# Softmax results and retention outputs transposed in 32x32 blocks by VectorE and moved over DRAM, in place of TensorE transposes

## The chip, the cores and the metric

The kernel runs on one core of one Trainium2 chip. The metric is device time in microseconds (us) for one execution of the whole program; lower is better. PE is TensorE, DVE is VectorE, ACT is ScalarE, POOL is GpSimd, and SP is the engine that only issues transfers (its queue is SPq in the trace).

## The reference, cut to what matters

Two layers of a block with neighbourhood attention and retention side by side, then a third block of another kind. Sequence 512, width 1024, all fp32. In each of the two layers the parts that the change touches are these:

```python
# neighbourhood attention: 8 heads of 64
s = einsum('bhcd,bhrckd->bhcrk', q_row, k_win) * scale + bias
pr = softmax(s)                                # one row per query
out = einsum('bhcrk,bhrckd->bhcd', pr, v_win)  # sums over keys
# bidirectional retention: 4 heads, values of 256
o = (o - mu) * rsqrt(var + GN_EPS)
yb = silu(g) * o
merged = sigmoid(gate_a) * (ya @ w_branch_a) + sigmoid(gate_b) * (yb @ w_branch_b)
```

The softmax is computed with queries on the 128 partitions, but the product with the values sums over keys, so keys must lie on the partitions there. The retention output is computed with tokens on the partitions, but `yb @ w_branch_b` sums over features. Both results have to be transposed in between.

## The kernel before, in words

Every product is made of three fp32r matmuls on a high and a low part of each operand (`mm3`). `split` (line 667) makes the two parts of a tile: ACT casts the high part, DVE subtracts it from the source for the low part. Weights come in as `raw` tiles of 512 KB and are split by the same two engines into `whi` and `wlo`; four `raw` buffers are shared by the weights and by `pth`/`ptl`.

In each layer the main line of PE's work is, in this order: `vg` of head 0, `q`, `k`, `v` of the attention, then for each of four retention heads `qr` and `vg`, then `ba`, `ga`, and pairs of `gb` and `bb`. Beside it run generators of side work: `attention()` (line 1167) and one `retention(h, qk)` (line 1255) per head. `attention()` must be finished before `ba`, which reads its result; the retention outputs are read only by `bb`.

For each of eight attention heads there are two halves (`gp`). A half is: four matmuls into a PSUM bank `s`; DVE adds the bias and takes the row maximum (`nmx`); ACT makes the exponential with its row sums; DVE takes the reciprocal and scales the tile `s_` (128x512, queries by keys). Then, at lines 1225 to 1230, PE transposes the four 128x128 blocks of `s_` into a PSUM bank `pt`, and `split` reads `pt` into `pth` and `ptl`. After both halves, eight matmuls `o` multiply `pth` and `ptl` with the values. In `retention`, the two tiles `yt` of a head (each 128x512, tokens by features) are transposed by PE at lines 1300 to 1306 into two banks `ybt` and split into `ybh` and `ybl`.

No engine's order is written by hand. All instructions are recorded by a `Planner`, which gives each a cost (`record`, line 309) and a due time, plays all engines through, and issues them in the order that it found. Each engine then runs its own list strictly in that order. The costs that matter here:

```python
if op.dma:
    op.cost = 1.0 if eng == "gpsimd" else 0.06
    op.set = n * o.ap[0][1] * 4 / 3.6e5
elif meth == "transpose":
    op.cost = 0.11
```

A transfer is taken to land 2.0 us after its bytes have passed, an instruction may follow one of another engine after `SYNC = 0.5`, and one of PE after `PE_SYNC = 1.5`.

Of the kernel before, what the change touches and what calls it, by code (L numbers as in the profile page):

```python
# [12 lines left out]
F32 = mybir.dt.float32  # L13
# [5 lines left out]
P = 128  # L19
# [487 lines left out]
def block_kernel(ctx: ExitStack, tc: tile.TileContext, keys, w, x, xt, pt, bias, decay, tabs, vecs,  # L507
# [16 lines left out]
    def nm(s):  # L524
        uid[0] += 1
        return f"{s}{uid[0]}"
# [4 lines left out]
    def tmp(s="tmp", dt=F32):  # L531
        return tp.tile([P, 512], dt, tag="tmp", name=nm(s))
# [7 lines left out]
    def psb(s="ps"):  # L540
        return pp.tile([P, 512], F32, tag="bg", name=nm(s), bufs=4)
# [4 lines left out]
    ident = cst.tile([P, P], F32, name="ident")  # L546
# [120 lines left out]
    def split(src, hi, lo):  # L667
        S.copy(out=hi, in_=src)
        V.tensor_tensor(out=lo, in0=src, in1=hi.bitcast(F32), op=ALU.subtract)
# [31 lines left out]
    def to_feature_half(src, xt_, t, hf):  # L701
# [6 lines left out]
        S.copy(out=h, in_=v)  # L708
        V.tensor_tensor(out=l, in0=v, in1=h.bitcast(F32), op=ALU.subtract)

    def bcast(r):
        b = [act(s="bc") for _ in range(2)]
        for hf in range(2):
            G.dma_start(out=b[hf], in_=rows[r:r + 1, hf * HALF:(hf + 1) * HALF].to_broadcast([P, HALF]))
        return b
# [30 lines left out]
    ps = psb("warm")  # L746
# [337 lines left out]
    for i in range(DEPTH):  # L1084
# [82 lines left out]
        def attention():  # L1167
# [14 lines left out]
            for f in range(4):  # L1182
# [5 lines left out]
                for h in (2 * f, 2 * f + 1):  # L1188
# [8 lines left out]
                    for gp in range(2):  # L1197
# [24 lines left out]
                        for u in range(2):  # L1222
                            V.tensor_scalar(out=s_[:, u * 256:u * 256 + 256], in0=s_[:, u * 256:u * 256 + 256],
                                            scalar1=sm[:, u:u + 1], scalar2=None, op0=ALU.mult)
                        pst = psb("pt")
                        for c in range(4):
                            src = c ^ 1 if gp == 1 and c > 1 else c
                            TE.transpose(out=pst[:, c * P:(c + 1) * P], in_=s_[:, src * P:(src + 1) * P], identity=ident)
                        ps2 = slice(512 * gp, 512 * gp + 512)
                        split(pst, pth[:, ps2], ptl[:, ps2])  # L1230
                        yield 2.2
                    po = psb("o")
                    for n in (1, 2, 3, 0):
# [21 lines left out]
        def retention(h, qk):  # L1255
# [41 lines left out]
            yield 1.0  # L1297
            while not att_done:
                yield 0.1
            for c in range(2):  # L1300
                ps = psb("ybt")
                for n in range(4):
                    TE.transpose(out=ps[:, n * P:(n + 1) * P],
                                 in_=yb[n // 2][:, 256 * (n % 2) + P * c:256 * (n % 2) + P * c + P], identity=ident)
                hi, lo = act(F32R, "ybh"), act(F32R, "ybl")
                split(ps, hi, lo)
                ybT[2 * h + c] = (hi, lo)
                yield 0.5

        att_done = []  # L1310
        att_gen = attention()
# [418 lines left out]
```

## Time and profile before

| | |
|---|---|
| Median of 3 runs | 2258.62 us (2257.99 to 2259.11) |
| The profiled execution, its own time | 2257.85 us |
| Its span | 2256.1 us |
| PE busy | 2228.9 us (99% of the span) |
| DVE busy | 1467.0 us (65%) |
| ACT busy | 1038.2 us (46%) |
| POOL busy | 635.1 us (28%) |

Times of instructions come from the one profiled execution; its own time is 1.75 us longer than its span, and 0.77 us shorter than the median. In the trace all instructions have line 503, where the planner issues them, so groups are told apart by the names of their tiles: `pt` are the softmax transposes, `ybt` those of the retention, `qks` the attention's operands moved by SP.

### The profile page before, as it was taken

To read this page: it belongs to the slowest core of one execution; us is meant where nothing else is said; L and a number is where in the kernel's file an instruction comes from. 1 tells how busy PE (TensorE), PEld (TensorE's weight loads), DVE (VectorE), ACT (ScalarE), POOL (GpSimd) and SP (SyncE) were. 2 spreads that over 40 slices of the span, in tenths; PEclk is the share of its full clock that TensorE was granted. 3 is DMA by queue.
4 is the path that set the end of the run, shared out by engine and by line. 5 is a ranking of instruction groups with operands and counts; after the bars stand their busy time and mean duration, and the time that the engine had idled before them with its cause. 6 is when DMAs were issued, how large, how long until landed. Compare 5 with 4: busy or idle time off the path is not lost.

```text
span 2256.1 us, 28362 instructions
## 1 busy us (share of the span) xinstructions
PE 2228.9 (99%) x10572; PEld 1863.2 (83%) x10572; DVE 1467.0 (65%) x2139; ACT 1038.2 (46%) x1680; POOL 635.1 (28%) x752
## 2 busy tenths in 40 slices
PE   9999999999999999999999999999999979999998
PEld 8888888888888888888888888888888868888887
DVE  4488734576887867277853474787887874566663
ACT  5378632244444444267752333544443674333332
POOL 0011011147437830011001136636761230221220
PEclk9999999999999999999999999999999999999999
DMA  7344333433333444444333433333343432333331
GB/s 242 88 125 144 121 94 94 141 100 122 121 101 102 124 138 135 121 127 134 115 94 100 159 101 104 98 116 101 121 143 119 145 120 77 103 103 103 103 99 51
DMA packets 85017, 262.14 MB, mean 116 GB/s; under 512 B 10880, under 2 KB 11024, under 8 KB 84880
## 3 DMA queue, kind: packets, MB, share of 16 engines
q1 hardware_dynamic: 79680, 242.16, 34.8%
q0 software_dynamic: 5200, 18.18, 2.7%
q8 instruction: 83, 1.36, 0.2%
q14 instruction: 54, 0.44, 0.1%
HBM read 235.13 MB, written 12.58 MB: 110 GB/s over the span
## 4 chain that ended last, share of the span: by engine, by line
PE 86%; DVE 6%; POOL 4%; ACT 2%; issue 1%; DMA 1%; DVEq 0%; SPq 0%; ACTq 0%; POOLq 0%
PE up L503 15%; PE tm L503 14%; PE vg L503 8%; PE fd L503 7%; PE u L503 6%; PE g L503 5%; PE ga L503 4%; PE bb L503 4%; PE gb L503 4%; PE qr L503 4%; PE ro L503 2%; PE ba L503 2%; PE k L503 2%; PE q L503 2%; PE v L503 2%; DVE wlo L503 2%
## 5 line engine op out<-in xcount | busy, mean ns | idle before, releaser
L503 DVE TENSOR_TENSOR wlo<-raw,whi 128x1024 fp32r<-128x1024 f32 (+1 forms) x372 | 497.7, 1345 | 337.2 <-ACT whi L503 334.9
L503 ACT CAST whi<-raw 128x1024 fp32r<-128x1024 f32 (+1 forms) x372 | 385.6, 1041 | 349.5 <-PE fd L503 74.8
L503 PE MATMUL up<-xtl,whi 128*128 128x512 f32 x704 | 271.2, 390 | 0.0
L503 PE MATMUL up<-xth,wlo 128*128 128x512 f32 x704 | 271.2, 390 | 0.0
L503 PE MATMUL up<-xth,whi 128*128 128x512 f32 x704 | 270.8, 389 | 0.0
L503 DVE SCALAR_TENSOR_TENSOR h<-up,vec,h 128x511 f32<-128x511 f32 x176 | 130.8, 745 | 88.0 <-ACT h L503 86.3
L503 PEld LDWEIGHTS up<-xth,whi 128*128 128x128 f32 x704 | 132.2, 188 | 27.3
L503 PEld LDWEIGHTS up<-xth,wlo 128*128 128x128 f32 x704 | 132.1, 188 | 27.4
L503 PEld LDWEIGHTS up<-xtl,whi 128*128 128x128 f32 x704 | 132.1, 188 | 27.2
L503 PE MATMUL fd<-whi,gh 128*128 128x512 f32 x336 | 132.3, 394 | 0.5 <-DVE mid L503 0.3
L503 PE MATMUL fd<-wlo,gh 128*128 128x512 f32 x336 | 132.2, 394 | 0.0
L503 PE MATMUL fd<-whi,gl 128*128 128x512 f32 x336 | 131.8, 392 | 0.0
L503 POOL TENSOR_TENSOR ws<-raw,raw 128x512 f32<-128x512 f32 x48 | 76.2, 1606 | 197.2 <-DMA raw<-in_w 197.2
L503 POOL TENSOR_TENSOR h<-h,h 128x512 f32<-128x512 f32 x44 | 78.2, 1777 | 160.3 <-DVE h L503 114.5
L503 ACT ACTIVATE h<-up,vec 128x512 f32<-128x512 f32 x88 | 68.0, 776 | 111.9 <-PE up L503 111.9
L503 POOL DMA_DIRECT2D bias<-in_bias x30 | 16.5, 549 | 321.9 <-DVE s L503 321.9
L503 PE MATMUL u<-xtl,whi 128*128 128x512 f32 (+1 forms) x288 | 101.4, 356 | 1.7 <-DVE xtl L503 1.7
L503 PE MATMUL u<-xth,wlo 128*128 128x512 f32 (+1 forms) x288 | 101.6, 356 | 0.0
L503 DVE TENSOR_TENSOR x<-x,fd 128x512 f32<-128x512 f32 x144 | 96.0, 680 | 8.4 <-PE fd L503 8.2
L503 PE MATMUL u<-xth,whi 128*128 128x512 f32 (+1 forms) x288 | 100.7, 356 | 0.0
L503 PE MATMUL vg<-whi,xtl 128*128 128x512 f32 x256 | 100.5, 395 | 0.0
L503 POOL TENSOR_TENSOR ws<-raw,ws 128x512 f32<-128x512 f32 x48 | 74.3, 1568 | 92.3 <-DMA raw<-in_w 92.2
(347 smaller groups left out, 5636.3 us busy)
## 6 DMA issues: line engine op xcount, KB each, us to landing
raw<-in_w SPq DMA_DIRECT2D x376, 512.0 KB, 3.9
bias<-in_bias POOLq DMA_DIRECT2D x30, 256.0 KB, 3.9
bc<-in_rows POOLq DMA_DIRECT2D x22, 256.0 KB, 6.4
qks<-kh SPq DMA_DIRECT2D x32, 128.0 KB, 2.4
qks<-kl SPq DMA_DIRECT2D x32, 128.0 KB, 2.4
dec<-in_tabs POOLq DMA_DIRECT2D x7, 448.0 KB, 3.6
raw<-in_w SPq DMA_DIRECT2D x8, 256.0 KB, 5.5
xr<-in_xt SPq DMA_DIRECT2D x8, 256.0 KB, 5.6
```

The source lines that it names most:

```text
L503: getattr(getattr(self.nc, op.eng), op.meth)(*op.args, **op.kw)
```

## The change

A new function `turn(src_, parts)` (line 711 of the changed file) takes the place of the transposes. DVE transposes the tile in blocks of 32x32 into a buffer `tb`: one instruction where the order of the key blocks is kept, three where the second half swaps two of them. SP writes `tb` to a DRAM tile `turn` (256 KB), then reads it back in four transfers of 64 KB, each to 32 partitions in runs of 512 bytes, into the tile that was the source. `split` then reads this tile in SBUF in place of a PSUM bank. In the retention the splits are made in halves of 256 columns. The PSUM banks `pt` and `ybt` are gone.

```diff
+    def turn(src_, parts):
+
+        b = tmp("tb")
+        for lo_, order in parts:
+            n = len(order)
+            v = src_.rearrange("p (c b j) -> p b c j", c=4, b=4)
+            V.transpose(out=b.rearrange("p (b c i) -> p b c i", b=4, c=4)[:, :, lo_:lo_ + n],
+                        in_=v[:, :, order[0]:order[0] + n])
+        d = dp.tile([P, 512], F32, name=nm("turn"))
+        Q.dma_start(out=d, in_=b)
+        for k in range(4):
+            Q.dma_start(out=src_[32 * k:32 * k + 32].rearrange("p (a n) -> p a n", a=4),
+                        in_=d.rearrange("(a j) (b n) -> b j a n", a=4, b=4)[k])
+        return src_.rearrange("p (a c i) -> p c a i", a=4, c=4)
...
-                        pst = psb("pt")
-                        for c in range(4):
-                            src = c ^ 1 if gp == 1 and c > 1 else c
-                            TE.transpose(out=pst[:, c * P:(c + 1) * P], in_=s_[:, src * P:(src + 1) * P], identity=ident)
+                        got = turn(s_, ((0, (0, 1, 2, 3)),) if gp == 0 else ((0, (0, 1)), (2, (3,)), (3, (2,))))
                         ps2 = slice(512 * gp, 512 * gp + 512)
-                        split(pst, pth[:, ps2], ptl[:, ps2])
+                        split(got, *(v[:, ps2].rearrange("p (c a i) -> p c a i", c=4, a=4) for v in (pth, ptl)))
...
+            got = [turn(yb[n2], ((0, (0, 1, 2, 3)),)) for n2 in range(2)]
+            yield 0.2
             for c in range(2):
-                ps = psb("ybt")
-                for n in range(4):
-                    TE.transpose(out=ps[:, n * P:(n + 1) * P],
-                                 in_=yb[n // 2][:, 256 * (n % 2) + P * c:256 * (n % 2) + P * c + P], identity=ident)
                 hi, lo = act(F32R, "ybh"), act(F32R, "ybl")
-                split(ps, hi, lo)
+                for n2 in range(2):
+
+                    split(got[n2][:, c:4:2], *(v[:, 256 * n2:256 * n2 + 256].rearrange("p (u a i) -> p u a i", u=2, a=4)
+                                              for v in (hi, lo)))
                 ybT[2 * h + c] = (hi, lo)
-                yield 0.5
+                yield 0.2
```

`V` is VectorE, `Q` is SP's queue. The planner orders everything anew, so most engines' lists differ from the attention on. Three places follow.

PE in the first layer, at the transposes of the first attention head, before (`pt` are the transposes, `qr` is the main line's product):

```order
L503 MATMUL qr183_272<-xth4_88,wlo108_197 128x512
L503 MATMUL pt147_236<-ident_78,s144_233 128x128 x4
L503 MATMUL qr183_272<-xth4_88,whi107_196 128x512
L503 MATMUL pt153_242<-ident_78,s150_239 128x128 x4
L503 MATMUL qr183_272<-xtl5_89,whi107_196 128x512
L503 MATMUL qr183_272<-xth4_88,wlo108_197 128x512
```

The same head now, at its first two `o` matmuls, the product with the values (`vg` is the next product of the main line):

```order
L503 MATMUL vg242_331<-whi181_270,xth4_88 128x512
L503 MATMUL o161_250<-pth140_229,vs122_211 128x256
L503 MATMUL vg242_331<-wlo182_271,xth4_88 128x512
L503 MATMUL vg242_331<-whi181_270,xtl5_89 128x512
L503 MATMUL vg242_331<-whi181_270,xth4_88 128x512
L503 MATMUL vg242_331<-wlo182_271,xth4_88 128x512
L503 MATMUL o161_250<-ptl141_230,vs122_211 128x256
```

The eight transposes of the head are gone. Between the last `s` matmul of the head's first half and its first `o` matmul stood 39 matmuls of 512 columns, 8 of 256 and the 8 transposes; now 61 of 512 and 12 of 256 stand there.

DVE in the first layer, third attention head, now (`tb` is the transposed tile, `s` the softmax tile, `sum` its reciprocals; the other rows are side and main work):

```order
L503 STREAM_TRANSPOSE tb224_313<-s221_310 128x512
L503 TENSOR_TENSOR pl229_318<-pf227_316,ph228_317 128x512
L503 TENSOR_TENSOR wlo239_328<-raw235_324,whi238_327 128x1024
L503 SCALAR_TENSOR_TENSOR s248_337<-s247_336,bias246_335 128x512
L503 TENSOR_REDUCE nmx249_338<-s248_337 128x2
L503 TENSOR_TENSOR ql302_391<-qn64_153,qh301_390 128x512
L503 TENSOR_TENSOR vl244_333<-vg257_346,vh243_332 128x256
L503 SCALAR_TENSOR_TENSOR pf254_343<-rs253_342,dec193_282 128x512
L503 RECIPROCAL sum250_339<-sum250_339 128x2
L503 TENSOR_SCALAR s248_337<-s248_337,sum250_339 128x256 x2
L503 STREAM_TRANSPOSE tb251_340<-s248_337 128x4x64
L503 STREAM_TRANSPOSE tb251_340<-s248_337 128x4x32 x2
```

Each half has its block transposes right behind its scaling: one for the first half, three for the second. The subtraction `ptl` of the first half, which needs the tile back from DRAM, stands 16 instructions behind its transpose.

SP in the first layer, fifth attention head, now (`turn` is the tile in DRAM, `s` the softmax tile that it is read back to, `raw` a weight tile; the brackets name the semaphores that a transfer waits for, those with DMAHW those of earlier transfers):

```order
L503 DMA turn316_405<-tb315_404 128x512 [waits DMAHW2_49,DVE_49]
L503 DMA turn323_412<-tb322_411 128x512 [waits DMAHW3_49,DVE_49]
L503 DMA s312_401<-turn316_405 32x4x128 [waits DMAHW4_49,DMAHW2_49]
L503 DMA s312_401<-turn316_405 32x4x128 [waits DMAHW5_49]
L503 DMA s312_401<-turn316_405 32x4x128 [waits DMAHW6_49]
L503 DMA s312_401<-turn316_405 32x4x128 [waits DMAHW7_49]
L503 DMA raw328_417<-in_w 128x1024 [waits DMAHW0_49]
L503 DMA raw329_418<-in_w 128x1024 [waits DMAHW1_49]
L503 DMA s319_408<-turn323_412 32x4x128 [waits DMAHW3_49]
L503 DMA s319_408<-turn323_412 32x4x128
L503 DMA s319_408<-turn323_412 32x4x128 [waits DMAHW4_49]
L503 DMA s319_408<-turn323_412 32x4x128 [waits DMAHW5_49]
```

Both halves are written, then the first is read back, then two weight tiles are fetched, then the second half is read back. The first read of a half waits for its write to have landed, and all that stands behind it on SP waits with it. SP issues five transfers for each `turn`, and there are 48 turns: 16 of the softmax and 8 of the retention in each layer.

## Rows read from the trace of the kernel before

**Rows 1.** Page, part 1: busy time, share and instructions of each engine.

```profile
PE 2228.9 (99%) x10572; PEld 1863.2 (83%) x10572; DVE 1467.0 (65%) x2139; ACT 1038.2 (46%) x1680; POOL 635.1 (28%) x752
```

**Rows 2.** Busy time by stretch (first `s` to `ba`; `ba` to `gb`; both layers).

```profile
core 0: us, PE busy (x) PEld busy (x) DVE busy (x) ACT busy (x) POOL busy (x), PEclk, DMA share, GB/s
101.00:253.00 152.00, 151.81 (x823) 129.51 (x822) 126.51 (x247) 113.29 (x211) 20.26 (x25) 1.00 0.47 136
253.00:331.00 78.00, 78.00 (x383) 65.51 (x383) 34.74 (x52) 38.79 (x60) 9.04 (x7) 1.00 0.32 99
980.00:1132.00 152.00, 151.97 (x826) 129.75 (x825) 124.23 (x242) 114.90 (x210) 17.72 (x22) 1.00 0.48 137
1132.00:1210.00 78.00, 78.00 (x380) 65.56 (x379) 32.56 (x45) 34.76 (x51) 10.34 (x8) 1.00 0.31 95
```

**Rows 3.** Waits of PE, longest first: waiter, releaser, us in total, times, longest.

```profile
PE sy L503 <- DVE st L503: 7.2, 5, 2.3
PE s L503 <- DMA qks<-kl: 0.2, 1, 0.2
```

**Rows 4.** The transposes: tiles `pt` and `ybt`, ns min/median/max, first and last start.

```profile
L503 PE MATMUL pt<-ident,s x128: 270/272/274, 109.9 to 1100.7; 128*128 128x128 f32 x128
L503 PE MATMUL ybt<-ident,yt x64: 270/272/273, 255.1 to 1166.3; 128*128 128x128 f32 x64
```

**Rows 5.** Chain that ended last, by time: start, us, what, times (pieces of first layer).

```profile
71.00 21.76 PE v L503 x96
113.61 0.48 PE s L503 x4
116.07 0.44 PE pt L503 x4
```

**Rows 6.** Timeline, first head: start, us, engine, instruction.

```profile
107.42 0.61 DVE L503 TENSOR_SCALAR s<-s,sum 128x256 f32<-128x256 f32 x2
109.92 0.60 PE L503 MATMUL pt<-ident,s 128*128 128x128 f32 x4
110.61 1.21 ACT L503 CAST pth<-pt 128x512 fp32r<-128x512 f32 x2 [1.44 <-PE pt L503]
113.10 0.28 PE L503 MATMUL o<-pth,vs 128*128 128x256 f32 x1
```

**Rows 7.** DVE groups, 101 to 253 us: count, busy us, mean ns, idle before, releaser.

```profile
L503 DVE TENSOR_TENSOR wlo<-raw,whi 128x1024 fp32r<-128x1024 f32 x17 | 20.7, 1220 | 2.9 <-ACT whi L503 2.9
L503 DVE TENSOR_TENSOR ptl<-pt,pth 128x512 fp32r<-128x512 f32 x16 | 10.9, 683 | 0.1
L503 DVE TENSOR_TENSOR vl<-vg,vh 128x256 fp32r<-128x256 f32 x11 | 4.6, 421 | 7.2 <-ACT sg L503 7.2
```

**Rows 8.** DVE group of 128 columns, 30 to 430 us, same columns.

```profile
L503 DVE COPY kn<-k 128x128 f32<-128x128 f32 x4 | 1.2, 292 | 12.1 <-PE k L503 12.1
```

**Rows 9.** Waits of DVE, 101 to 253 us, same columns as rows 3.

```profile
DVE vl L503 <- ACT sg L503: 7.2, 5, 2.5
DVE pf L503 <- PE rs L503: 4.9, 5, 1.9
DVE wlo L503 <- ACT whi L503: 2.9, 4, 1.0
```

**Rows 10.** Transfers, whole span: count, KB each, median us from issue to landing.

```profile
raw<-in_w SPq DMA_DIRECT2D x376, 512.0 KB, 3.9
qks<-kh SPq DMA_DIRECT2D x32, 128.0 KB, 2.4
x_d<-x SPq DMA_DIRECT2D x8, 256.0 KB, 2.1
x<-x_d SPq DMA_DIRECT2D x8, 256.0 KB, 4.2
```

**Rows 11.** What SP takes to issue one, ns min/median/max (tiles `x_d` and `qks`).

```profile
L503 SPq DMA_DIRECT2D x_d<-x x8: 319/323/327, 858.9 to 883.9; - x8
L503 SPq DMA_DIRECT2D qks<-kl x32: 461/568/1538, 59.3 to 1082.1; - x32
```

**Rows 12.** First use of the retention outputs (tile `ybh`).

```profile
L503 PE MATMUL bb<-ybh,whi x128: 389/389/389, 341.7 to 1289.0; 128*128 128x512 f32 x128
```

**Rows 13.** Stretches of the third block in which PE waits, columns as rows 2.

```profile
1780.00:1800.00 20.00, 16.65 (x90) 13.33 (x88) 19.83 (x28) 12.04 (x31) 5.55 (x6) 1.00 0.32 101
1800.00:1850.00 50.00, 37.50 (x190) 31.08 (x191) 39.62 (x57) 39.19 (x93) 15.33 (x13) 0.91 0.39 127
```

## The prediction

> **What bounds the kernel now.** I read the busy shares first. PE is busy 2228.9 us of 2256.1 [rows 1], so time is saved only by taking work from PE, and lost wherever PE comes to wait. The waits of PE say where it waits today: in the third block, 7.2 us for `st` and a few more; in the two layers the longest wait for a side operand is 0.2 us, for `qks` [rows 3]. Then I cut the span at the places of the change. From the first `s` to the first `ba` PE is busy 151.8 of 152 us in the first layer and 152.0 of 152 in the second; DVE 126.5 and 124.2, which is 83% and 82%, and far above its 65% over the span; ACT 113.3 and 114.9 [rows 1, 2]. Behind it, from `ba` to `gb`, DVE is busy 34.7 of 78 us. The reader is to see that the softmax transposes leave a full PE and land on the engine that is fullest beside it.
>
> **What is removed.** 128 transposes `pt` and 64 `ybt` [rows 4]. One of them lasts 270 ns, but PE overlaps its instructions: in the chain four take 0.44 us, so 0.11 us each; a matmul of 512 columns takes 21.76 / 96 = 0.227 us, one of 256 takes 0.12 us [rows 5]. PE has no gap there, so 192 x 0.11 = 21.1 us is what the span can lose: 14.1 us by the softmax (7.0 in each layer's first stretch), 7.0 us by the retention.
>
> **What DVE gets.** No block transpose stands in the trace. It reads one tile and writes one, so by its size the nearest rows are `ptl`, 683 ns for 512 columns, `vl`, 421 ns for 256, and a copy of 128 columns, 292 ns [rows 7, 8]. I take 0.68 us for the whole tile and 0.42 + 2 x 0.29 = 1.00 us where three instructions do it. The upper end is 1.22 us, the row of 1024 columns [rows 7], for a transpose that passes its data twice. In the stretch of a layer stand 16 softmax turns and, by the new order, 4 of the retention: 8 x 0.68 + 8 x 1.00 + 4 x 0.68 = 16.2 us. The subtractions `ptl` stay as long, now from SBUF. The stretch itself gets shorter, 152 - 7.0 = 145 us of PE work. So DVE has 126.5 + 16.2 = 142.7 us to do in 145, and 140.4 in the second layer. It can't be busy all that time. Its waits for PE, like 4.9 us for `rs`, vanish once it is late, but those for ACT stay, since ACT's order stays: 7.2 us in `vl`, the largest, and 2.9 in `wlo` [rows 9]. With 7.2 us, DVE needs 149.9 and 147.6 us: PE waits for it 4.9 + 2.6 = 7.5 us. With no such idle it waits for nothing. The planner doesn't see this: it books any `transpose` at 0.11 us, also DVE's, and so packs DVE's list as if 16.2 us were some 4.
>
> **What the way over DRAM adds.** On PE the `o` matmuls need the turned tile. Before, in the first head, scaling ends at 108.03 us, `pt` starts 1.9 us later and takes 0.60, the two casts end at 111.82, and `o` starts 1.3 us later [rows 6]: 3.2 us of margin. Now: block transpose 0.68; write, 2.1 us from issue to landing (`x_d<-x`); three reads issued ahead of the last one, 0.32 to 0.57 us each [rows 11]; the last read, 2.4 us (`qks`, small, within SBUF) to 4.2 us (`x<-x_d`, from DRAM) [rows 10]. Together 6.1 to 8.7 us, less PE's 0.60: 5.5 to 8.1 more, in the second half 0.3 more still. The new order gives part of it: counted with the 0.227, 0.12 and 0.11 us above, PE's work between the `s` of a first half and its first `o` goes from 12.0 to 16.1 us as a mean of the eight heads, and from 10.7 to 16.1 us for the second half. So the first half is short by 5.5 - 4.1 - 3.2 = -1.8 to +0.8 us, the second by -2.7 to +0.1. Mostly it fits. At the upper end 16 heads x 0.8 = 12.8 us are lost; I take 2.5, a fifth, since the middle of the range has slack.
>
> The Trainium skill gives one transfer a fixed 2.0 us plus its bytes at 436 GB/s ("DMA: Bandwidth & Descriptors", section "Anatomy of one DMA", fitted for transfers that GpSimd issues): estimates of 2.6 us for the write and 2.15 for a read, and by it no head would be short and the time 2.5 us less than my sum. The rows differ both ways: 2.1 us for a write of the same size, 4.2 for a read.
>
> **What I cost at nothing.** The retention turns: the first `bb` is at 341.7 us [rows 12], 89 us behind `ba`, and DVE is free more than half of the time there [rows 2]; without that cover each of 16 would cost its 6.1 to 8.7 us. ACT: `pth` comes from SBUF, some 0.04 us longer, 16 times in a stretch in which ACT is free 39 us. SP: 100 transfers more in a stretch, 32 to 57 us of issuing, and a wait of about 2.1 us at each pair's write; queued behind those waits are weight tiles, whose buffers SP fills ahead of use. Bytes: 20 turns move 10.5 MB beside 20.7 MB (136 GB/s x 152 us), a DMA share of 0.47 that becomes some 0.7. POOL's queue keeps its bias loads. Clock: the granted clock is 1.00 (2.4 GHz) even where PE idles 3.4 of 20 us, and 0.91 where it idles 12.5 of 50 [rows 13]; 5 us in 145 should not lower it.
>
> **The sum**, against the profiled execution's own 2257.85 us: -21.1 + 7.5 + 2.5 = -11.1, so 2246.8 us. That execution is 0.77 us under the median of the runs; I say 2247. Ends of the unknown costs: no wait at all, 2236.8; both at their ends (ACT's idle 10.1 us: 13.3, and 12.8), 2262.9.
>
> **Rivals.**
>
> 1. *Nothing waits.* For it: before, DVE's list was full too and PE waited 0.2 us; a late DVE also absorbs its idle, 25.5 us now. Against it: the 2.3 us that would be left. 2236.8 us.
>
> 2. *DVE becomes the bound, and the change loses.* If a block transpose of 512 columns takes 1.22 us, DVE gets 16.2 x 1.22 / 0.683 = 28.9 us in each stretch, PE waits 17.6 + 15.3 = 32.9 us, and with the 2.5 the time is 2272. It decides from 0.92 us per transpose, where the waits eat the 21.1 us. For it: 98% load, and a list packed for 0.11 us. Against it: all DVE instructions here that pass 512 columns once take about 0.68 us. The Trainium skill speaks for this side ("VectorE: DVE Perf Modes", sections "The three transpose paths" and "Rules for kernel authors"): a 128x128 transpose belongs on TensorE if PSUM will do as its destination, and it states 390 ns there and 311 ns for VectorE's blocks, bf16; four times 311 ns would be an estimate of 1.24 us, and a time of about 2273. In this trace TensorE's cost is 0.11 us of PE's time, less than a third of that figure.
>
> 3. *Landings come late on PE.* SP puts two weight tiles between the reads of the two halves of a head, and a tile of 512 KB lands 1.5 us later than one of 128 KB (3.9 against 2.4) [rows 10]. If each head is short by 0.8 + 1.5 = 2.3 us, 16 heads cost 36.8 us: 2257.85 - 21.1 + 36.8 = 2273.6 (DVE catches up in these waits, so its 7.5 isn't added). It decides from 1.3 us per head. For it: the DMA share near 0.7, and reads that wait on SP behind a write. Against it: such weight loads stand in the middle of few heads, and two heads often wait at the same time.
>
> **How the numbers follow.** No change means within 0.2%, 2254.1 to 2263.1 us, about what a measurement of this kernel can tell. My forecast, waits of 3 to 17 us in sum (2240 to 2254), has 0.40. Nothing waits (below 2240): 0.24. Waits of 17 to 25 us, which give back about all: 0.14. Rival 2: 0.11; rival 3: 0.11. So faster 0.64, the same 0.14, slower 0.22. The range runs from just below rival 1 to 2268, where it leaves out most of rivals 2 and 3, 2 in 10: 2235 to 2268.
>
> **What would show it.** In the profile of the changed kernel: no `pt` or `ybt`, PE's busy time near 2208 us; `STREAM_TRANSPOSE` of 512 columns near 0.68 us (1.2 would be rival 2); DVE over 95% busy from `s` to `ba`, and that stretch near 150 us; PE waiting some 5 us per layer, with `ptl`, `pl` or `wlo` from DVE as releasers (with `pth` behind a landing of `s`: rival 3); reads of `turn` landing in 2.4 to 4.2 us; nothing waiting for `ybh`. A stretch of 155 us or more, or a granted clock below 1.00 in it, would make the prediction wrong.

## The result, and the profile after

The changed kernel takes 2285.57 us (median of 4 runs, 2281.01 to 2288.09) against 2258.86: a ratio of 1.0115, 95% interval 1.0103 to 1.0127. It is slower by 27 us; the forecast was 2247 us, 11 us faster, and its range ended at 2268. The profiled execution took 2284.95 us, with a span of 2283.2.

The page, part 1, of the changed kernel; it answers to [rows 1]:

```profile
PE 2228.3 (98%) x10380; PEld 1856.0 (81%) x10380; DVE 1501.2 (66%) x2235; ACT 1035.3 (45%) x1690; POOL 633.4 (28%) x752
```

The 192 transposes are gone (10572 to 10380 instructions), and yet PE is as busy as before: 2228.3 us against 2228.9. Its idle time, span less busy time, went from 27.2 to 54.9 us. So two things were lost, not one: 27.7 us of new idle time, and 20.5 us by which PE was busy longer than the 21.1 us of removed work would have it. Together 48.2 us, less the 21.1, is the 27.1 us by which the span grew.

The same stretches as [rows 2], same columns, of the changed kernel:

```profile
101.00:253.00 152.00, 140.00 (x687) 116.99 (x686) 128.32 (x260) 101.08 (x195) 19.41 (x24) 0.94 0.62 176
253.00:331.00 78.00, 75.94 (x374) 63.68 (x374) 47.53 (x86) 47.55 (x80) 7.00 (x6) 1.00 0.52 165
980.00:1132.00 152.00, 141.58 (x690) 118.17 (x690) 126.76 (x258) 100.91 (x196) 19.27 (x24) 0.93 0.59 168
1132.00:1210.00 78.00, 74.60 (x371) 62.23 (x370) 49.22 (x90) 48.94 (x81) 5.71 (x5) 1.00 0.58 173
```

A PE that was full waits 12.0 and 10.4 us in the two attention stretches, the granted clock there is 0.94 and 0.93, and DVE is at 84 and 83%, not over 95%: it too waits, so its capacity alone is not what binds. All the new idle time came in these four cuts: 12.0 + 2.1 + 10.4 + 3.4 = 27.9 us.

The waits of PE from 0 to 1300 us, columns as [rows 3], longest first:

```profile
PE o L503 <- ACT pth L503: 5.9, 5, 3.0
PE s L503 <- DMA qks<-kh: 5.6, 2, 2.8
PE vg L503 <- ACT rb L503: 5.0, 4, 2.0
PE o L503 <- DVE ptl L503: 4.3, 3, 1.7
PE ro L503 <- ACT ph L503: 3.1, 4, 1.1
PE vg L503 <- ACT whi L503: 2.4, 3, 0.9
```

Only the first and the fourth have to do with the turned tile. `qks` comes late over SP's queue, and `rb`, `ph` and `whi` come late from ACT, which had hardly anything added to its list (1690 instructions for 1680). What SP waits for from 101 to 253 us, same columns:

```profile
SPq L503 <- PE s L503: 45.0, 3, 31.7
SPq L503 <- DVE tb L503: 19.8, 10, 4.5
...
SPq L503 <- DMA raw<-in_w: 5.6, 4, 2.5
...
SPq L503 <- DMA turn<-tb: 4.3, 4, 1.8
```

And ACT, in the same stretch:

```profile
ACT whi L503 <- DMA raw<-in_w: 11.5, 8, 3.1
ACT pth L503 <- DMA s<-turn: 5.1, 5, 2.3
```

The first row is old: in the kernel before, SP waited 85.7 us of this stretch for PE to be done with an operand. So SP is not full over the stretch as a whole. New are the 19.8 us at writes whose block transposes DVE has not yet made, and the 4.3 us until a write has landed. ACT waited 6.6 us for `raw` in the kernel before; now it is 11.5. This is SP's own timeline (start, us, instruction) in the 16 us before the first long gap of PE:

```profile
121.69 1.83 SPq L503 DMA_DIRECT2D s<-turn  x4
123.94 1.10 SPq L503 DMA_DIRECT2D qks<-qh  x2
125.09 2.02 SPq L503 DMA_DIRECT2D s<-turn  x4
127.16 0.90 SPq L503 DMA_DIRECT2D raw<-in_w  x2
128.16 1.35 SPq L503 DMA_DIRECT2D qks<-ql  x2
129.61 2.47 SPq L503 DMA_DIRECT2D qks<-kh  x4
132.52 3.41 SPq L503 DMA_DIRECT2D qks<-kl  x2
136.04 1.01 SPq L503 DMA_DIRECT2D raw<-in_w  x2
```

SP issues almost without a pause here; one wait of 2.5 us, for a weight tile to land, lies inside the row at 132.52. The operands of the next head stand behind the reads of the last one and behind two weight tiles. They are also slow to land. The four `kh` issued from 129.61 us, and the same four in the kernel before, where no weight tile stands just ahead of them (columns as [rows 10]; before, then after):

```profile
qks<-kh SPq DMA_DIRECT2D x4, 128.0 KB, 2.3
qks<-kh SPq DMA_DIRECT2D x4, 128.0 KB, 6.6
```

PE gets them 2.8 us late:

```profile
137.10 0.55 PE L503 MATMUL s<-qks,qks 128*128 128x256 f32 x1 [2.79 <-DMA qks<-kh]
```

Last, what a run of gaps does to the matmuls behind it (PE's timeline of the changed kernel: start, us, instruction, idle time before it and releaser in brackets):

```profile
179.99 0.39 PE L503 MATMUL o<-ptl,vs 128*128 128x256 f32 x1 [0.91 <-DVE ptl L503]
181.02 0.38 PE L503 MATMUL o<-pth,vs 128*128 128x256 f32 x1 [0.65 <-ACT pth L503]
182.47 0.80 PE L503 MATMUL vg<-whi,xth 128*128 128x512 f32 x1 [1.07 <-ACT rb L503]
183.07 0.63 PE L503 MATMUL vg<-wlo,xth 128*128 128x512 f32 x1
183.50 0.63 PE L503 MATMUL vg<-whi,xtl 128*128 128x512 f32 x1
...
187.12 0.63 PE L503 MATMUL vg<-whi,xtl 128*128 128x512 f32 x1
187.55 0.41 PE L503 MATMUL ro<-vh,ph 128*128 128x256 f32 x1
...
188.53 0.39 PE L503 MATMUL vg<-wlo,xth 128*128 128x512 f32 x1
```

After 2.6 us of idle time in three gaps PE runs from 182.5 to 188 us at the lower of its two levels, 1.2 GHz (the granted clock of that stretch is 0.50): a matmul of 512 columns starts 0.43 us after the last one instead of 0.23. In the stretches of both layers 52 matmuls of 512 columns last over 0.55 us and 35 of 256 over 0.40; in the kernel before there is none.

### The profile page after: what moved, and what is told of

Its sections match the earlier page's. It is cut to its first block, busy times and chain, and to the rows that moved or that the text cites. A ratio compares the mean times of both kernels' runs of the same rounds, so it can differ in the third digit from the quotient of the medians.

```text
span 2283.2 us, 28590 instructions
## 1 busy us (share of the span) xinstructions
PE 2228.3 (98%) x10380; PEld 1856.0 (81%) x10380; DVE 1501.2 (66%) x2235; ACT 1035.3 (45%) x1690; POOL 633.4 (28%) x752
## 4 chain that ended last, share of the span: by engine, by line
PE 42%; DVE 5%; POOL 2%; ACT 2%; DMA 1%; issue 1%; SPq 0%; DVEq 0%; ACTq 0%; POOLq 0%
PE tm L503 8%; PE up L503 8%; PE u L503 6%; PE fd L503 5%; PE g L503 5%; PE bb L503 2%; PE gb L503 2%; PE ga L503 2%; DVE wlo L503 1%; PE ba L503 1%; DMA raw<-in_w 1%; DVE z L503 1%; ACT yt L503 1%; DVE x L503 1%; POOL ws L503 0%
## 5 line engine op out<-in xcount | busy, mean ns | idle before, releaser
L503 PEld LDWEIGHTS up<-xth,whi 128*128 128x128 f32 x704 | 132.2, 188 | 27.2
L503 PEld LDWEIGHTS up<-xth,wlo 128*128 128x128 f32 x704 | 132.2, 188 | 27.2
L503 PE MATMUL vg<-whi,xth 128*128 128x512 f32 x256 | 103.0, 412 | 7.7 <-ACT rb L503 5.0
L503 POOL TENSOR_TENSOR ra<-ra,rb 128x512 f32<-128x512 f32 x16 | 21.4, 1336 | 317.1 <-DVE rb L503 297.6
L503 PE MATMUL vg<-wlo,xth 128*128 128x512 f32 x256 | 103.7, 406 | 0.0
```

The source lines that it names most:

```text
L503: getattr(getattr(self.nc, op.eng), op.meth)(*op.args, **op.kw)
```

## The experiments

Theories after the result: SP's queue holds back what else it carries (A); DVE's block transposes make DVE late (B); the turned tiles come late on the path of `o` (C). The first four kernels keep the changed kernel's order on every engine; a tag on the planner's records tells the turn's instructions apart when they are issued. Where the blocks or the transfers are left out, the tiles reach the splits without that part of their transposition. In the fences `...` marks lines left out. The kernel before took 2258.51 us beside them.

**Block transposes kept, no transfers.**

```diff
             for op in order:
+                if op.tag in ("write", "read"):
+                    continue
```

> The changed kernel with its order of all engines kept, but without the transfers of a turn: none of the 48 writes to DRAM and 192 reads back is issued; the block transposes on VectorE stay. Left out: the blocks are not moved to their places, so the tiles that are split hold the softmax and retention results as they were. Theory A (SP's queue: the five transfers of each turn clog it, so that attention operands, weight tiles and the turned tiles arrive late) and theory C (the way over DRAM is longer than the order leaves room for): PE's waits for pth, ptl, qks, rb, whi in the two layers are gone, the granted clock is back at 0.99 or more, time 2238 to 2248 us. Theory B (the block transposes overload VectorE, as the prediction had it): the waits stay, time 2270 us or more.

Measured: 2265.39 us, 1.0032 (1.0020 to 1.0044), in the range of neither theory. The transfers are worth 20.2 us, but without them the kernel still isn't faster than before.

**Transfers kept, no block transposes** (the write takes the scaled tile).

```diff
+                if op.tag == "blocks":
+                    continue
+                if op.tag == "write":
+                    op.kw["in_"] = self.other[op.n]
```

> The changed kernel with its order kept, but without the 80 block transposes on VectorE: the softmax and retention tiles are written to DRAM themselves and read back as before. Left out: the transposition within blocks. Theory B: VectorE is relieved of 16 us in each attention stretch, PE's waits are gone, time 2240 to 2252 us. Theories A and C: all transfers stay, so the waits stay, time 2272 to 2290 us; at most the 1 us by which each tile reaches DRAM earlier is gained.

Measured: 2273.07 us, 1.0066 (1.0051 to 1.0081). The lower end of A and C, and 12.5 us under the changed kernel: B has its part too.

**Neither.**

```diff
+                if op.tag in ("blocks", "write", "read"):
+                    continue
```

> The changed kernel with its order kept, without transfers and without block transposes: the whole turn is left out, the splits read the tiles as they are. All three theories: 192 transposes of 0.11 us are gone from PE and nothing takes their place, time 2236 to 2243 us. If it is 2255 us or more, the new order itself loses the time, whatever the turn costs.

Measured: 2247.60 us, 0.9954 (0.9937 to 0.9970), a miss. Even with nothing in the place of the transposes the new order returns 10.9 of the 21.1 us. The three give one table (page, part 1, and the span; the sum of PE's work without the transposes is 2228.9 - 21.1 = 2207.8 us):

| kernel | time | PE idle | PE busy | busy above 2207.8 |
|---|---|---|---|---|
| neither | 2247.60 | 32.9 | 2212.6 | 4.8 |
| blocks alone | 2265.39 | 43.5 | 2219.9 | 12.1 |
| transfers alone | 2273.07 | 46.5 | 2224.7 | 16.9 |
| changed kernel | 2285.57 | 54.9 | 2228.3 | 20.5 |

Over "neither", the blocks cost 17.8 us, the transfers 25.5, both 38.0. In each row the busy time rises with the idle time. The waits of PE in the two layers (us) say which part brings which wait:

| PE waits for | neither | blocks alone | transfers alone | changed kernel |
|---|---|---|---|---|
| `pth` | 0 | 1.2 | 3.5 | 5.9 |
| `ptl` | 1.1 | 5.7 | 0.5 | 4.3 |
| `qks` | 1.1 | 4.2 | 5.8 | 5.6 |
| `rb` | 2.6 | 5.0 | 4.2 | 5.0 |
| `ph` and `whi` | 0 | 0 | 5.9 | 5.5 |

`ph` and `whi` come late with the transfers alone, `ptl` with the blocks alone. `rb` and `qks` come late with either: part of that is the new order, which puts two weight tiles just ahead of those four `kh` in all four kernels, where they take 6.0 us or more to land (medians).

**The turn's transfers issued by GpSimd.**

```diff
-                getattr(getattr(self.nc, op.eng), op.meth)(*op.args, **op.kw)
+                eng = "gpsimd" if op.tag in ("write", "read") else op.eng
+                getattr(getattr(self.nc, eng), op.meth)(*op.args, **op.kw)
```

> The changed kernel with its order kept, but the five transfers of each turn are issued by GpSimd's queue and not by SP's; nothing is left out. Theory A: SP is free for the attention operands and weight tiles, whose waits on PE (qks, rb, whi, 13 us) go; time 2245 to 2265 us, the rest being GpSimd's own work standing behind waits. Theory C: the way over DRAM is as long as before, the waits for pth and ptl stay, time 2278 to 2292 us. Theory B: no change, 2280 to 2290 us.

Measured: 2313.63 us, 1.0246 (1.0231 to 1.0261): no theory had this. The waits of PE of this kernel, whole span:

```profile
PE o L504 <- ACT pth L504: 33.6, 12, 5.5
...
PE vg L504 <- ACT rb L504: 5.7, 4, 2.5
```

No `s` waits for `qks` any more (5.6 us in the changed kernel). This looks like A's mark and is not: SP issues those four `kh` from 128.88 us, 0.7 us earlier than in the changed kernel, and they take 7.5 us to land; PE comes to them only at 143.1 us, after two waits for `pth` have held it for 6.9 us. GpSimd takes 0.55 us for each of the 240 transfers and has a list of its own, in which these transfers stand behind other waits, and now PE waits 33.6 us for `pth`. The queue was exchanged, not removed.

The next four (kernel before beside them: 2258.56 us).

**All transfers, but read back aside**, to a DRAM tile that nobody reads, so that ACT, DVE and PE wait for no landing of a turn.

```diff
+                if op.tag == "read":
+                    op.kw["out"] = self.other[op.n]
...
+        aside = dp.tile([P, 512], F32, name=nm("aside"))
...
+            plan_.other[plan_.ops[-1].n] = aside[32 * k:32 * k + 32].rearrange("p (a n) -> p a n", a=4)
```

> Edit: every instruction of the changed kernel in its order, all 240 transfers of the turns issued by SP with their sizes and their waits on the writes, but the four reads of a turn land in an unused DRAM tile, and the splits read the scaled tile as it is, so nothing on ACT, DVE or PE waits for a landing of a turn. The softmax results and retention outputs are thus left untransposed. The transfers cost the changed kernel some 20 us (2285.57 against 2265.39 without them). Theory L (their landings come late on the path of the o matmuls): the time falls to that without transfers, 2263 to 2270 us, and PE's wait of o for pth falls from 5.9 us to about 1. Theory Q (what costs is SP's queue: 100 more issues and the waits on the writes hold back weight tiles and qks): 2278 to 2288 us, PE's wait for qks stays near 5.6 us. In between: both, in that proportion.

Measured: 2290.66 us, 1.0140 (1.0124 to 1.0155). PE's wait of `o` for `pth` fell to 1.3 us as expected, and the time didn't fall: against L, and 2.7 us above the range of Q. PE now waits 8.4 us for `whi` and 5.2 for `ph`. One flaw showed in its trace: a read to DRAM took SP 598 ns to issue, against 430 in the changed kernel. So later the reads were sent into the turn's own tile `tb` in SBUF instead (kernel before beside it: 2260.04 us).

```diff
-            plan_.other[plan_.ops[-1].n] = aside[32 * k:32 * k + 32].rearrange("p (a n) -> p a n", a=4)
+            plan_.other[plan_.ops[-1].n] = b[32 * k:32 * k + 32].rearrange("p (a n) -> p a n", a=4)
```

> Edit: as the kernel whose turns land aside (2290.66 us), but the four reads of a turn land in its own tile tb in SBUF, not in DRAM: there a read took SP 598 ns to issue, in the changed kernel 430 ns, so that kernel gave SP 13 us more to do in a stretch than the changed one has. The splits still read the scaled tile as it is; softmax results and retention outputs are left untransposed. Theory Q (SP's queue): 2278 to 2287 us, as the changed kernel's 2285.57. Theory L (landings on the path, hidden so far by the dearer issues): 2264 to 2273 us.

Measured: 2297.05 us, 1.0163 (1.0146 to 1.0180), at 430 ns a read, 10 us above the range of Q. It has a flaw of its own: `tb` is held until the read has landed, and ACT's `qh` now waits 3.8 us and DVE's next `tb` 2.4 for such a landing. Neither run gives theory L anything, but each brings a cost of its own, so that a few us of it can't be excluded, and neither meets Q's number.

**The planner told what a transfer and a block transpose cost.**

```diff
-            op.cost = 1.0 if eng == "gpsimd" else 0.06
+            op.cost = 1.0 if eng == "gpsimd" else 0.43
-            op.cost = 0.11
+            op.cost = 0.11 if eng == "tensor" else 0.15 + n / 960.0
```

> Edit: two costs of the planner alone: a transfer on SP 0.43 us in place of 0.06, a transpose on DVE 0.15 us + columns / 960 in place of 0.11; the planner then orders everything anew. Theory O (the order is at fault: DVE's and SP's lists are packed for costs that are a sixth of the true ones): PE's idle time falls from 54.9 us to 35 to 42 and the clock follows, 2248 to 2262 us. Theory K (capacity: in the stretches DVE has 143 us of work for 145 and every landing takes its time, so no order helps): 2272 to 2290 us.

Measured: 2285.65 us, 1.0116 (1.0096 to 1.0137), what the changed kernel takes, with 55.1 us of idle time for 54.9. Theory O, which said 35 to 42, is out: told these two costs, with 16 softmax turns in a stretch, this planner finds no better list. That no list would do, as K says, is not shown.

**The retention outputs by turn, the softmax on PE.**

```diff
-                        got = turn(s_, ((0, (0, 1, 2, 3)),) if gp == 0 else ((0, (0, 1)), (2, (3,)), (3, (2,))))
+                        pst = psb("pt")
+                        for c in range(4):
+                            src = c ^ 1 if gp == 1 and c > 1 else c
+                            TE.transpose(out=pst[:, c * P:(c + 1) * P], in_=s_[:, src * P:(src + 1) * P], identity=ident)
...
-                        split(got, *(v[:, ps2].rearrange("p (c a i) -> p c a i", c=4, a=4) for v in (pth, ptl)))
+                        split(pst, pth[:, ps2], ptl[:, ps2])
```

> Edit: the softmax tiles are transposed by PE as before, the retention outputs by turn. Takes 64 x 0.11 = 7.0 us from PE. Theory R (what costs is the softmax turns, which PE waits for within a head; the retention has time until bb): 2251 to 2254 us. Rival (any turn in the full stretch costs DVE time and SP issues that PE pays for): four of eight retention turns of a layer fall into that stretch, 2257 to 2264 us.

Measured: 2259.26 us, 1.0002 (0.9992 to 1.0011): the rival. The 7.0 us are gained and lost again, 2.5 and 2.1 us of it as idle time of PE in the two stretches.

**The softmax by turn, the retention on PE** (the mirror of the edit above, at lines 1300 to 1306).

> Edit: the retention outputs are transposed by PE as before, the softmax tiles by turn. Takes 14.1 us from PE. Theory R: the whole loss of the changed kernel stays, less the 7.0 us that the retention gave: 2288 to 2294 us. Rival: without the four retention turns in the stretch DVE has 2.7 us less to do and SP 20 transfers less, PE waits less, 2270 to 2282 us.

Measured: 2280.31 us, 1.0097 (1.0082 to 1.0112): the rival again. The softmax turns bring 21.8 of the 27 us of loss; the retention turns of the changed kernel cost 5.3 us more than the 7.0 they save.

Two kernels ask what of SP's queue costs (kernel before beside these two and the one behind them: 2259.20 us). Both go out from the one that reads back aside, 2290.66 us.

**An eighth of the bytes** (64 columns of `tb` to a DRAM tile `few`, and quarters of it to another).

```diff
+                if op.tag in ("write", "read"):
+                    op.kw.update(self.small[op.n])
```

> Edit: as the kernel whose turns land aside (2290.66 us), but each turn's write moves 32 KB in place of 256 and each of its four reads 8 KB in place of 64; SP issues as many transfers, in the same places, and each write still waits for DVE's block transposes and the first read for the write. Softmax results and retention outputs are left untransposed. Theory W (SP stands at the writes' waits for DVE, and weight tiles and qks behind them come late) and theory N (240 more issues of SP by 0.3 to 0.57 us): no change, 2284 to 2293 us. Theory B (the bytes: a DMA share of 0.6 in place of 0.47 makes every landing later): 2263 to 2272 us.

Measured: 2286.22 us, 1.0117 (1.0102 to 1.0132). The DMA share of the first stretch fell from 0.59 to 0.44, the time by 4.4 us, in the range of W and N: bytes are a small part. SP takes 587 ns to issue such a read of 8 KB, and took 598 for one of 64.

**No waits** (the writes take the constant `cos_t`, the reads the input `bias`).

```diff
+                if op.tag in ("write", "read"):
+                    op.kw.update(self.free[op.n])
```

> Edit: as the kernel whose turns land aside (2290.66 us), with all bytes, but the writes take a constant tile and the reads an input, so that none of the 240 transfers waits for DVE or for another transfer of the turn. Softmax results and retention outputs are left untransposed. Theory W: SP's 17 us of waits for tb in a first stretch go, weight tiles and qks come in time, 2263 to 2274 us. Theories N and B: 2283 to 2293 us.

Measured: 2275.60 us, 1.0071 (1.0056 to 1.0086), 15.1 us less, though SP issues as many transfers and each write takes it longer (546 ns for 338). This is theory W, 1.6 us above its range, and against N and B. PE's waits behind late weight tiles fell with it: `vg` for `whi` from 8.4 to 2.8 us, `ro` for `ph` from 5.2 to none. (DVE waits for no free `tb` in either kernel, so that is not the reason.) `qks`, which W expected in time, came as late as before: 6.1 us for 6.2. In the changed kernel itself `whi` and `ph` are 5.5 us of PE's waits, not 13.6, so how much of the 15.1 us the waits of SP cost there is not shown. Against the kernel without transfers (2265.39) some 10 us are left: the bytes' 4.4, and 6 or so that the mere issues would take, which no run shows alone.

**Retention by turn, with the true costs.** Both edits above together.

> Edit: softmax on PE, retention outputs by turn, and the planner told 0.43 us for a transfer on SP and 0.15 us + columns / 960 for a transpose on DVE. Theory: with few turns in the full stretch there is room for a list that is packed for true costs, PE's idle time falls from 30.2 us back to 27, and the time to 2251 to 2255 us. Rival: true costs move nothing here either (they moved nothing with all turns), 2257 to 2261 us.

Measured: 2250.14 us, 0.9958 (0.9941 to 0.9975): faster than both kernels, a little beyond the theory's range. First stretch of each layer, columns as [rows 2], and the page's part 1:

```profile
101.00:253.00 152.00, 151.98 (x826) 130.22 (x825) 129.23 (x253) 118.22 (x218) 20.12 (x25) 1.00 0.53 150
980.00:1132.00 152.00, 151.97 (x824) 130.22 (x824) 127.78 (x248) 120.26 (x216) 15.90 (x21) 1.00 0.53 150
```

```profile
PE 2221.8 (99%) x10508; PEld 1858.8 (83%) x10508; DVE 1476.5 (66%) x2171; ACT 1045.8 (47%) x1700; POOL 634.6 (28%) x752
```

PE is full again, at full clock, and its busy time is 7.1 us under the 2228.9 of before: 64 x 0.11, all of it, though such a number can be off by some 2.5 us (the control below, with all its transposes, has 2231.4); its idle time is 26.1 us for 27.2. That the costs alone don't do it is shown by the control:

**The kernel before, SP's transfers at 0.43 us in the planner.** (Kernel before beside this and the next two: 2259.36 us.)

```diff
-            op.cost = 1.0 if eng == "gpsimd" else 0.06
+            op.cost = 1.0 if eng == "gpsimd" else 0.43
```

> Edit: the kernel before, with TensorE transposes everywhere, and the planner told 0.43 us for a transfer on SP in place of 0.06. A control for the version with retention turns and true costs (2250.14 us). Theory (the gain of that version is the 7.0 us of ybt that PE no longer does, and the costs only keep it from being lost): no change, 2256 to 2261 us, PE's idle time near 27 us. Rival (the costs alone give the gain, the turns nothing): 2249 to 2253 us.

Measured: 2257.81 us, 0.9994 (0.9985 to 1.0003), no change. The turns of the retention give the gain, and with the costs it comes through, as far as one list of the planner for each kernel can show it.

The last two ask whether idle time by itself makes PE slower, in the kernel before and away from the crowded stretches.

**18 gaps in PE's work.** In the planner's `issue`, ahead of a matmul whose operand PE used one or two matmuls earlier, DVE copies this operand six times onto itself:

```diff
+            at, last = [340.0 + 16 * j for j in range(9)] + [1220.0 + 16 * j for j in range(9)], []
...
+                if at and rhs is not None and op.start > at[0] and key in last and rhs.ap[-1][1] == 512:
+                    at.pop(0)
+                    v = rhs.bitcast(F32)
+                    for _ in range(6):
+                        self.nc.vector.tensor_copy(out=rhs, in_=v)
```

> Edit: the kernel before in its order; at 18 places of the two stretches behind the retention, where PE is 100% busy, DVE copies an operand of the next matmul six times onto itself, after PE's last use of it and before the next, so that PE waits. No transfer is added, and no work of PE. By the copy of 128 columns, 292 ns, and ptl, 683 ns, a gap is 1.5 to 4 us, in sum 27 to 72 us of idle time. Theory C (the idle time by itself lowers the granted clock): PE's busy time rises from 2228.9 us by 0.5 to 0.9 of the idle time added, and the clock in rows behind a gap is under 1.00. Rival (it was the load of DMA and DVE in the full stretch): busy time stays within 3 us of 2228.9.

Measured: 2339.52 us, 1.0353 (1.0338 to 1.0368). PE is idle for 76.3 us, 49.1 more, 2.7 a gap, and busy for 2262.4, 33.5 more: 0.68 of the idle time, theory C. The two stretches, and PE behind one gap:

```profile
331.00:500.00 169.00, 148.20 (x615) 119.33 (x614) 88.37 (x128) 41.66 (x54) 17.23 (x16) 0.94 0.31 95
1220.00:1420.00 200.00, 177.15 (x732) 143.25 (x732) 102.80 (x140) 51.07 (x68) 35.50 (x41) 0.93 0.30 94
```

```profile
363.99 0.39 PE L513 MATMUL gb<-xtl,whi 128*128 128x512 f32 x1
366.98 0.50 PE L513 MATMUL gb<-xth,wlo 128*128 128x512 f32 x1 [2.60 <-DVE xth L510]
367.31 0.53 PE L513 MATMUL gb<-xth,whi 128*128 128x512 f32 x1
367.64 0.63 PE L513 MATMUL gb<-xtl,whi 128*128 128x512 f32 x1
...
370.63 0.49 PE L513 MATMUL gb<-xth,wlo 128*128 128x512 f32 x1
370.96 0.39 PE L513 MATMUL gb<-xth,whi 128*128 128x512 f32 x1
```

The DMA share is 0.31 there and DVE is at 52%, and the granted clock is the same 0.94 and 0.93 as in the changed kernel's stretches; in the kernel before it is 1.00 in both. Matmuls at 1.2 GHz follow 15 of the 18 gaps, 6 to 12 at a time. No crowd is needed.

**54 short gaps** (one copy for six, at 54 places).

> Edit: as the kernel with 18 gaps, but one copy in place of six, at up to 54 places. A gap is 0.3 to 1 us, in sum 16 to 54 us. Theory C1 (each us of idle time lowers the clock alike, in short gaps and long): busy time rises by 0.5 to 0.9 of the idle time added. Rival C2 (short gaps cost themselves alone): busy time rises by less than 0.2 of it.

Measured: 2304.10 us, 1.0197 (1.0180 to 1.0214). Idle time is 27.5 us more, 0.5 a gap, and busy time 18.9 more, again 0.69 of it, as theory C1 says. But the clock is not the reason here:

```profile
331.00:500.00 169.00, 158.14 (x682) 122.83 (x681) 87.90 (x134) 53.18 (x73) 20.00 (x16) 1.00 0.34 108
1220.00:1420.00 200.00, 184.28 (x788) 143.92 (x787) 96.94 (x126) 55.33 (x75) 45.09 (x57) 0.99 0.32 99
```

At a clock of 1.00 and 0.99 each gap adds 18.9 / 54 = 0.35 us of busy time. One of the gaps shows most of it:

```profile
343.62 0.39 PE L513 MATMUL bb<-ybl,whi 128*128 128x512 f32 x1
344.31 0.50 PE L513 MATMUL bb<-ybh,wlo 128*128 128x512 f32 x1 [0.29 <-DVE ybh L510]
344.64 0.39 PE L513 MATMUL bb<-ybh,whi 128*128 128x512 f32 x1
```

In the stream a matmul lasts 0.39 us and the next starts 0.23 us after it. The one ahead of the gap runs its last 0.16 us alone, and the one behind the gap is followed after 0.33 us instead of 0.23: the overlap is lost, and the trace books it as busy. (The profile models where a matmul ends; measured are the 0.69 us between the two starts across the gap, 0.46 more than in the stream, of which it books 0.29 as idle.) So a gap has three prices: its idle time, 0.35 us, and for some the slower clock behind it. By these prices, as an estimate, the changed kernel's 20.5 us split up so: 23 gaps x 0.35 = 8 us; 52 matmuls x 0.2 and 35 x 0.09 (0.213 for 0.12 us) = 14 us.

The Trainium skill says the like of the middle one ("TensorE: Matmul & The Clock Gate", section "Step-by-step: what each phase is for"): the drain of a matmul hides behind the next, and an isolated matmul can't hide it. The trace agrees, with the 0.16 us ahead of the gap.

## Why the prediction was wrong, step by step

- **The miss in one sum.** The time is 38.6 us above the 2247 that were forecast. The waits of PE came to 27.7 us where the sum had 10.0, which makes 17.7; the other 20.5 us are PE's longer busy time, a term that the sum did not have.
- **The 21.1 us on PE were right.** 0.11 us for each transpose: in the version with retention turns 64 fewer take 7.1 us off PE's busy time.
- **The price of a block transpose was right, and rival 2's doubling was not.** `STREAM_TRANSPOSE` in the changed kernel, whole span (columns as [rows 7]), softmax and retention:

```profile
L503 DVE STREAM_TRANSPOSE tb<-s 128x512 f32<-128x512 f32 x16 | 11.4, 712 | 0.5
L503 DVE STREAM_TRANSPOSE tb<-yt 128x512 f32<-128x512 f32 x16 | 11.1, 701 | 0.3
L503 DVE STREAM_TRANSPOSE tb<-s 128x128 f32<-128x128 f32 x32 | 7.4, 270 | 0.0
L503 DVE STREAM_TRANSPOSE tb<-s 128x256 f32<-128x256 f32 x16 | 7.0, 438 | 0.0
```

  0.71 us for the tile, and 0.44 + 2 x 0.27 = 0.98 for three pieces, where 0.68 and 1.00 were taken. The estimate of 1.24 us from the Trainium skill ("VectorE: DVE Perf Modes", section "The three transpose paths": four times its 311 ns) doesn't hold for these fp32 tiles. Its rule that a 128x128 transpose belongs on TensorE (same page, section "Rules for kernel authors") came out so for the softmax tiles (2280.31 us with their turns alone) and not for the retention's (2250.14), though not by that price.
- **"PE waits for late DVE", 7.5 us, was mis-sized.** Blocks alone cost 17.8 us over "neither": 10.6 us more idle time of PE, not 7.5, and 7.3 us more busy time, which the sum had no term for. The picture behind it was off too: DVE did not come to be full, it is busy 138.5 of the 167 us from the first `s` to `ba`, or 83%, and yet late where PE needed it (`ptl`).
- **The step that failed first: "SP ... queued behind those waits are weight tiles, whose buffers SP fills ahead of use", costed at nothing.** The transfers, with 2.5 us in the sum for all that they bring, are worth 20.2 us in the changed kernel, and 25.5 where the blocks are left out. PE waits 5.5 us for `ph` and `whi`, which it does not without them. SP's waits, taken away in the kernel that reads aside, gave 15.1 us back; that it is as much in the changed kernel is not shown. The cover was named (tiles fetched ahead) but not measured: ACT's wait for `raw`, 6.6 us already before, and the 0.2 us that PE waited for `qks` already then [rows 3], said that there was little of it. Of such waits the Trainium skill says ("DMA: Bandwidth & Descriptors", section "Anatomy of one DMA") that a wait on a semaphore is made on the issuing sequencer, ahead of dispatch. The trace agrees, with 19.8 us of SP standing for `tb`.
- **"The way over DRAM", 2.5 us, and rival 3.** Landings came as forecast (the write 2.1 us, a softmax read 2.2, a retention read 3.7). PE's wait for `pth` is 5.9 us, more than the 2.5 and far from rival 3's 36.8. Taking the landings off the path of `o` made nothing faster, in two runs that each had a cost of their own, so what the 5.9 us weigh stays open. Rival 3 named the right neighbourhood, reads that wait on SP behind a write, but only one of the victims: what stands behind them on SP comes late as well.
- **The second step that failed: the clock at nothing, and a gap at its length.** "5 us in 145 should not lower it" holds for 5 us: with nothing in the turns' place PE idles 4.2 and 3.2 us of 152, and the granted clock is 1.00. But the waits were longer, and neither the sum nor its upper ends nor rivals 2 and 3, with 33 and 37 us of waits, put more than its length on a gap. It cost 20.5 us here, by the estimate above some 8 at 0.35 us a gap and the rest by the clock. The share of idle time alone does not tell when the clock falls. 54 gaps of 0.5 us, 6 and 8% of their stretches, left it at 1.00 and 0.99; the changed kernel's idle time, 8 and 7% of its two attention stretches, lies in fewer and longer gaps and went with 0.94 and 0.93; in the third block 3.4 of 20 us left it at 1.00 [rows 13].
- **What had no term: the new order itself.** With nothing in the turns' place PE waits 5.7 us more than before, which with its busy time is half of the expected gain. Why, isn't settled: the waits are small and many (`vg` for `rb` 2.6 us, `rs` for `s` 1.3). The order also has the two weight tiles ahead of the four `kh`, which land after 6.0 us in this kernel and after 2.3 in the kernel before. True costs cured such waits only with few turns.
- **The two signs of being wrong were well chosen.** From the first `s` to `ba` it took 151.9 us in the first layer and takes 166.9 (104.12 to 271.04 us), where 150 was forecast and 155 named as the limit, at a clock under 1.00. Of the other marks, DVE over 95% busy and PE's busy time near 2208 us did not come.

## What to carry to other kernels

When a step moves off a full engine onto transfers, go through the queue that issues them as if it were an engine: each wait on it is a wait of everything behind, so look at what stands there and how early it is fetched. Look also at what stands just ahead of small operands in it: behind two weight tiles they took 6.6 us to land here, and 2.3 without. A gap in a full TensorE costs more than its length, here some 1.7 times; a sum that counts idle time alone is too small by that. Move the part that has slack (the retention outputs, 7 us gained once the planner knew the prices), and leave the part that its consumer waits for.

## What the runs showed of the hardware

- The issue of one transfer of 64 KB took SP 430 ns (median) into SBUF and 598 ns into DRAM, and GpSimd 552 ns into SBUF; one of 8 KB into DRAM took SP 587. The median landing of the reads into SBUF was 2.2 us for the softmax and 3.7 for the retention by SP, 2.5 and 4.0 by GpSimd; into DRAM it was 2.5.
- The issue of a write of 256 KB took SP 338 ns in the changed kernel, and 546 ns (median) in the kernel where it waited for nothing and took a constant tile; why is not shown.
- A gap of 0.5 us on TensorE costs 0.86 us in all (46.4 us of span for 54), one of 2.7 us 4.6 (82.6 for 18). Matmuls at 1.2 GHz followed 15 of the 18 long gaps, 6 to 12 at 0.43 us each. In the stretches of the short gaps the clock was 1.00 and 0.99.
- A block transpose of VectorE, fp32 and within SBUF, took 0.27, 0.44 and 0.71 us for 128, 256 and 512 columns.
